# One weight sum of the gate-and-up product taken from two transfers: a plain load and an accumulating load

## The chip, the cores and the metric

The kernel runs on one core of one Trainium2 chip, as one program. The metric is the device time of that program in microseconds (us), measured on the chip. The profile used below is one separately profiled execution; times in it count from the start of its span. Its names for the engines are PE (TensorE, the matmul engine), DVE (VectorE), ACT (ScalarE), POOL (GpSimd) and SP (SyncE, which in this kernel issues the transfers between DRAM and on-chip memory).

## The reference

One layer of a hybrid encoder over 512 tokens of width 2048. The first part (two mixers behind one input projection, an output projection) is not touched by the change. The second part is a SwiGLU feed-forward network with 5632 hidden columns:

```python
h = rms_norm(x, norm2_g[layer]) * (1.0 + sc2) + sh2
gate, up = jnp.split(h @ w_ffn_in[layer], 2, axis=-1)
x = x + g2 * ((jax.nn.silu(gate) * up) @ w_ffn_out[layer])
```

All values are float32. `w_ffn_in` is 2048 by 11264: 5632 gate columns and 5632 up columns.

## The kernel before

Every matmul operand is split into a high part, which the matmul takes exactly, and a low part, the remainder (`S.copy` makes the high part on ScalarE, `V.tensor_sub` the low part on VectorE); a product is three matmuls per 128 rows of the contraction: high by high, high by low, low by high.

The first feed-forward product works on tiles f = 0 to 43 of 128 gate columns and the 128 up columns that belong to them. Tiles 0 and 1 are made in the plain way. Tiles 2 to 43 (lines 1004 to 1036) use a seven-product scheme of the Strassen-Winograd kind: the weights of a tile are four blocks of 1024 rows by 128 columns, A11 and A12 (gate, lower and upper half of the 2048 rows) and A21 and A22 (up, the same halves). On chip each is a tile of 128 partitions by 1024 values, 512 KB. Four sums of them are needed: S1 = A21 + A22, then A11 - A21 (kept in A21's place), S1 - A11 (kept in A11's place), and A12 minus that (in A12's place). The matching sums of the activations are made once, ahead of the loop (opA to opD in the profile).

The seven products of a tile run on TensorE in a fixed order, 24 matmuls of 128 by 256 each. In the profile they are told by their weights: ff_1 (A11 as loaded), ff_2 (A12 as loaded), ff_6 (S1 - A11), ff_7 (A11 - A21), ff_5 (S1), ff_4 (A22), ff_3 (the fourth sum). Each needs its weights split by `operand` (lines 880 to 886: ScalarE's cast at L884 makes ff_6h, VectorE's subtraction at L885 makes ff_6l). High and low parts have three buffers each, so a cast waits until the product three before it has been multiplied. Results are combined on VectorE (L1029, L1031, L1032, L990) and stored to DRAM by `keep` (L994, `actd`) for the second feed-forward product (`fo` in the profile).

Loads are issued by SP, in one queue and in order; `load_block` (L888 to 891) is the load of one block. A11 and A12 come from a pool of four buffers ("raw"), shared with the modulation weights (`ada`, L176) that are reduced on VectorE beside the first 16 or so tiles. A21, A22 and S1 come from a pool of five buffers ("raw2"). A transfer into a buffer waits on SP until the buffer's last user is done, and whatever stands behind it in SP's queue waits too.

The order on each engine is not the order of the code: a list scheduler of the framework places the instructions by priority and its own estimates of when operands are there, and gives out the buffers. The high-priority block moves splits and sums 300 steps ahead. The order that results is fixed in the program: an engine whose next instruction waits lets nothing pass.

Of the kernel before, what the change touches and what calls it, by code (L numbers as in the profile page):

```python
# [15 lines left out]
ALU = mybir.AluOpType  # L16
# [3 lines left out]
KT = 16  # L20
# [5 lines left out]
HALF = 8  # L26
# [102 lines left out]
def trunk(ctx, tc, a):  # L129
    nc = tc.nc  # L130
    V, S, G = nc.vector, nc.scalar, nc.gpsimd
# [11 lines left out]
    def acc(name):  # L143
        return psum.tile([P, T], F32, tag="acc", name=name)

    def att(name):
        return psum.tile([P, T], F32, tag="att", name=name, bufs=2)
# [732 lines left out]
    def operand(raw, name):  # L880
        hi = wp.tile([P, HALF, P], F32R, tag="hi", name=name + "h")
        lo = wp.tile([P, HALF, P], F32R, tag="lo", name=name + "l")
        with tc.high_priority(offset=AHEAD):
            S.copy(hi, raw)  # L884
            V.tensor_sub(lo, raw, hi.bitcast(F32))  # L885
        return hi, lo

    def load_block(pool, tag, bufs, f, g, kh):  # L888
        r = pool.tile([P, HALF, P], F32, tag=tag, name=f"ff{f}_{g}{kh}", bufs=bufs)
        nc.sync.dma_start(r, a["w_fi"][f, g][:, kh * HALF:kh * HALF + HALF])  # L890
        return r

    def product(out, w, p, first=False):
        whi, wlo = w
        for j in range(HALF):
            PE.matmul(out, whi[:, j], H[p][:, j, 0], start=first and j == 0, stop=False, skip_group_check=True)
            PE.matmul(out, whi[:, j], H[p][:, j, 1], start=False, stop=False, skip_group_check=True)
            PE.matmul(out, wlo[:, j], H[p][:, j, 0], start=False, stop=j == HALF - 1, skip_group_check=True)
# [83 lines left out]
    def tap(src, name):  # L982
        t = tp.tile([P, HT], F32, tag="tap", name=name, bufs=4)
        S.copy(t, src)
        return t
# [3 lines left out]
    def keep(f, sg, up):  # L989
        V.tensor_mul(sg, sg, up)  # L990
        pair = tp.tile([P, 2, T], F32R, tag="pair", name=f"pair{f}")
        S.copy(pair[:, 0], sg)
        V.tensor_sub(pair[:, 1], sg, pair[:, 0].bitcast(F32))
        nc.sync.dma_start(actd[f], pair.bitcast(F32))  # L994
# [9 lines left out]
    for f in range(2, FM):  # L1004
        A11, A12 = (load_block(wp, "raw", 4, f, 0, kh) for kh in range(2))
        A21, A22 = (load_block(tp, "raw2", 5, f, 1, kh) for kh in range(2))
        S1 = tp.tile([P, HALF, P], F32, tag="raw2", name=f"ffS{f}", bufs=5)
        A, B, C = acc(f"ffA{f}")[:, 0:HT], acc(f"ffB{f}")[:, 0:HT], att(f"ffC{f}")[:, 0:HT]
        w1, w2 = operand(A11, f"ff{f}_1"), operand(A12, f"ff{f}_2")
        with tc.high_priority(offset=AHEAD):  # L1010
            V.tensor_add(S1, A21, A22)
            V.tensor_sub(A21, A11, A21)
            V.tensor_sub(A11, S1, A11)
            V.tensor_sub(A12, A12, A11)
        product(A, w1, 1, True)
        ta = tap(A, f"a{f}")
        product(B, w2, 2, True)
        product(A, operand(A11, f"ff{f}_6"), 6)
        tb = tap(A, f"b{f}")
        product(C, operand(A21, f"ff{f}_7"), 7, True)  # L1020
        t_c = tap(C, f"c{f}")
        product(A, operand(S1, f"ff{f}_5"), 5)
        tu = tap(A, f"u{f}")
        product(C, operand(A22, f"ff{f}_4"), 4)
        product(A, operand(A12, f"ff{f}_3"), 3)

        sg = tp.tile([P, T], F32, tag="sg", name=f"sg{f}")
        up = tp.tile([P, T], F32, tag="up", name=f"up{f}")
        V.tensor_add(sg[:, 0:HT], B, ta)  # L1029
        S.activation(sg[:, 0:HT], sg[:, 0:HT], AF.Silu)  # L1030
        V.tensor_add(up[:, HT:T], tu, t_c)  # L1031
        V.tensor_add(up[:, 0:HT], C, tb)  # L1032
        S.activation(sg[:, HT:T], A, AF.Silu)
        keep(f, sg, up)
        if rest:
            rest.pop(0)()
# [98 lines left out]
```

## Time and profile before

| what | value |
|---|---|
| time, median of 2 runs | 2404.47 us (2404.03 to 2404.9) |
| the profiled execution's own time | 2405.08 us |
| its span | 2403.3 us |
| TensorE busy | 2321.8 us, 97% of the span |
| VectorE busy | 1701.3 us, 71% |
| ScalarE busy | 1033.9 us, 43% |
| GpSimd busy | 82.6 us, 3% |
| transfers, mean over the span | 168 GB/s |

The loop of tiles 2 to 43 lies between about 1067 us and 1921 us of the span. Busy time is time in which an engine had an instruction running; matmuls overlap, so their busy time alone does not tell how fast they run. An entry such as `<-DMA ff<-in_w_fi` behind an idle time names what ended it. In the chain of waits, followed back from the last instruction, each piece of time is given to the engine that it was spent on. "us to landing" of a transfer is the median time from its issue to its arrival. In the lists of order further below, the bracket names the counters for which an instruction waits: DMAHW for transfers issued by SP, DMASW for those issued by GpSimd, the others for engines.

### The profile page before, as it was taken

To read this page: it belongs to the slowest core of one execution; us is meant where nothing else is said; L and a number is where in the kernel's file an instruction comes from. 1 tells how busy PE (TensorE), PEld (TensorE's weight loads), DVE (VectorE), ACT (ScalarE), POOL (GpSimd) and SP (SyncE) were. 2 spreads that over 40 slices of the span, in tenths; PEclk is the share of its full clock that TensorE was granted. 3 is DMA by queue.
4 is the path that set the end of the run, shared out by engine and by line. 5 is a ranking of instruction groups with operands and counts; after the bars stand their busy time and mean duration, and the time that the engine had idled before them with its cause. 6 is when DMAs were issued, how large, how long until landed. Compare 5 with 4: busy or idle time off the path is not lost.

```text
span 2403.3 us, 36514 instructions
## 1 busy us (share of the span) xinstructions
PE 2321.8 (97%) x14371; PEld 2106.9 (88%) x14371; DVE 1701.3 (71%) x2585; ACT 1033.9 (43%) x1833; POOL 82.6 (3%) x64
## 2 busy tenths in 40 slices
PE   7989898999999999989999999999999999999999
PEld 6778788978888778889999999999999988888887
DVE  8997888789888875598888877777777633333332
ACT  4343664466565522374444444444444421122221
POOL 2250000000000200000000000000000000000000
PEclk9999999999999999999999999999999999999999
DMA  8878546743332286535555533333333484363342
GB/s 316 278 248 262 191 156 224 238 165 115 106 106 97 79 266 219 188 121 178 185 184 185 182 135 131 129 130 130 131 132 132 170 327 155 101 198 95 106 127 88
DMA packets 122488, 403.10 MB, mean 168 GB/s; under 512 B 13614, under 2 KB 14284, under 8 KB 122188
## 3 DMA queue, kind: packets, MB, share of 16 engines
q1 hardware_dynamic: 122316, 400.77, 49.8%
q8 instruction: 112, 1.84, 0.3%
q14 instruction: 60, 0.49, 0.1%
HBM read 369.24 MB, written 31.47 MB: 167 GB/s over the span
## 4 chain that ended last, share of the span: by engine, by line
PE 75%; DVE 10%; DMA 9%; issue 3%; ACT 2%; POOL 0%; POOLq 0%; SPq 0%; ACTq 0%; DVEq 0%
PE ffA L92 20%; PE fo L92 20%; PE ffC L92 10%; PE wo L92 6%; PE ffB L92 5%; DMA ada<-in_w_ada 4%; PE hgg L92 3%; DVE ada L183 3%; PE hgf L92 3%; PE hgq L92 3%; PE ff L92 1%; DMA fix<-in_w_fix 1%; DVE I L413 1%; PE l L92 1%; PE hgo L92 1%
## 5 line engine op out<-in xcount | busy, mean ns | idle before, releaser
L183 DVE SCALAR_TENSOR_TENSOR ada<-ada,cond 128x1024 f32<-128x1024 f32 x192 | 260.5, 1366 | 94.9 <-DMA ada<-in_w_ada 94.6
L92 PE MATMUL fo<-act,wfo_0h 128*128 128x512 f32 x1024 | 315.4, 389 | 0.0
L92 PEld LDWEIGHTS fo<-act,wfo_0h 128*128 128x128 f32 x1024 | 192.2, 188 | 39.9
L92 PE MATMUL fo<-act,wfo_0l 128*128 128x512 f32 x512 | 199.2, 389 | 0.0
L204 DVE TENSOR_TENSOR wfo_8l<-wfo_8r,wfo_8h 128x512 fp32r<-128x512 f32 x48 | 33.2, 692 | 177.6 <-ACT wfo_8h L203 177.6
L1071 DVE SCALAR_TENSOR_TENSOR x<-fo,mod,x 128x512 f32<-128x512 f32 x64 | 48.1, 751 | 131.2 <-PE fo L92 127.2
L203 ACT CAST wfo_0h<-wfo_0r 128x1024 fp32r<-128x1024 f32 x64 | 67.7, 1058 | 164.9 <-PE fo L92 142.1
L92 PE MATMUL ffA<-opA,ff_1h 128*128 128x256 f32 x672 | 124.6, 286 | 6.1 <-DVE up L1001 6.1
L92 PE MATMUL ffA<-opB,ff_6h 128*128 128x256 f32 x672 | 124.0, 285 | 2.1 <-ACT ff_6h L884 2.1
L92 PE MATMUL ffC<-opB,ff_7h 128*128 128x256 f32 x672 | 123.1, 283 | 0.4 <-ACT ff_7h L884 0.4
L92 PE MATMUL ffB<-opA,ff_2h 128*128 128x256 f32 x672 | 122.8, 283 | 0.0
L92 PE MATMUL ffA<-opC,ff_5h 128*128 128x256 f32 x672 | 122.8, 283 | 0.0
L92 PE MATMUL ffC<-opC,ff_4h 128*128 128x256 f32 x672 | 122.8, 283 | 0.0
L92 PE MATMUL ffA<-opD,ff_3h 128*128 128x256 f32 x672 | 122.8, 283 | 0.0
L203 ACT CAST wfo_8h<-wfo_8r 128x512 fp32r<-128x512 f32 x48 | 30.0, 624 | 210.3 <-PE fo L92 210.3
L92 PE MATMUL fo<-act,wfo_8h 128*128 128x512 f32 x384 | 118.2, 389 | 0.0
L92 PEld LDWEIGHTS fo<-act,wfo_0l 128*128 128x128 f32 x512 | 96.1, 188 | 19.9
L92 PEld LDWEIGHTS ffA<-opA,ff_1h 128*128 128x128 f32 x672 | 106.4, 195 | 6.3 <-issue 6.3
L92 PEld LDWEIGHTS ffA<-opB,ff_6h 128*128 128x128 f32 x672 | 105.9, 194 | 2.3 <-ACT ff_6h L884 2.3
L92 PEld LDWEIGHTS ffC<-opB,ff_7h 128*128 128x128 f32 x672 | 104.9, 192 | 0.7 <-ACT ff_7h L884 0.7
L92 PEld LDWEIGHTS ffB<-opA,ff_2h 128*128 128x128 f32 x672 | 104.8, 192 | 0.0
L92 PEld LDWEIGHTS ffA<-opC,ff_5h 128*128 128x128 f32 x672 | 104.8, 192 | 0.0
(691 smaller groups left out, 6727.1 us busy)
## 6 DMA issues: line engine op xcount, KB each, us to landing
ada<-in_w_ada SPq DMA_DIRECT2D x192, 512.0 KB, 4.5
ff<-in_w_fi SPq DMA_DIRECT2D x168, 512.0 KB, 3.6
wfo_0r<-in_w_fo SPq DMA_DIRECT2D x64, 512.0 KB, 3.6
actd<-pair SPq DMA_DIRECT2D x44, 512.0 KB, 2.6
act<-actd SPq DMA_DIRECT2D x44, 512.0 KB, 6.2
fix<-in_w_fix SPq DMA_DIRECT2D x28, 512.0 KB, 4.9
wfo_8r<-in_w_fo SPq DMA_DIRECT2D x48, 256.0 KB, 2.7
wo_8r<-in_w_out SPq DMA_DIRECT2D x16, 512.0 KB, 4.4
```

The lines of the kernel that those rows point to most:

```text
L92: self.engine.matmul(out, lhsT, rhs, **kw)
L183: V.scalar_tensor_tensor(w, w, 1.0, row[:, sl], op0=ALU.mult, op1=ALU.mult, accum_out=col)
L203: S.copy(hi, r)
L204: V.tensor_sub(lo, r, hi.bitcast(F32))
L413: V.tensor_tensor_scan(Ig[:, ::-1], seg[:, base:base + width][:, ::-1], Lg[:, ::-1], 0.0, op0=ALU.mult, op1=ALU.add)
L1071: V.scalar_tensor_tensor(x2[m], out, mcol(G2, m), x2[m], op0=ALU.mult, op1=ALU.add)
```

## The change

S1 is no longer added on VectorE. SP loads the upper half A22 from DRAM into S1's buffer a second time, and GpSimd then issues a transfer of the lower half A21 from DRAM that is added to what stands in that buffer. A21 and A22 are still loaded as before, for ff_7 and ff_4.

```diff
         A11, A12 = (load_block(wp, "raw", 4, f, 0, kh) for kh in range(2))
         A21, A22 = (load_block(tp, "raw2", 5, f, 1, kh) for kh in range(2))
         S1 = tp.tile([P, HALF, P], F32, tag="raw2", name=f"ffS{f}", bufs=5)
+        nc.sync.dma_start(S1, a["w_fi"][f, 1][:, HALF:KT])
+        nc.gpsimd.dma_start(S1, a["w_fi"][f, 1][:, 0:HALF], accum_op=ALU.add)
         A, B, C = acc(f"ffA{f}")[:, 0:HT], acc(f"ffB{f}")[:, 0:HT], att(f"ffC{f}")[:, 0:HT]
         w1, w2 = operand(A11, f"ff{f}_1"), operand(A12, f"ff{f}_2")
         with tc.high_priority(offset=AHEAD):
-            V.tensor_add(S1, A21, A22)
             V.tensor_sub(A21, A11, A21)
             V.tensor_sub(A11, S1, A11)
             V.tensor_sub(A12, A12, A11)
```

Lines behind the new ones move by one: the sum S1 - A11 is L1013 before and L1014 after, A11 - A21 is L1012 before and L1013 after.

The lists below are for VectorE and SP at one place well inside the loop, where no `ada` loads are left. Names: ff_00, ff_01, ff_10, ff_11 are A11, A12, A21, A22; ffS is S1; the number behind a name belongs to its tile f.

SP before, from one tile's first block to the next but one:

```order
L890 DMA ff_00_17489<-in_w_fi 128x1024 [waits DMAHW7_49,DVE_49]
L890 DMA ff_10_17493<-in_w_fi 128x1024 [waits DMAHW1_49,DVE_49]
L890 DMA ff_11_17495<-in_w_fi 128x1024 [waits DMAHW2_49,DVE_49]
L890 DMA ff_01_17491<-in_w_fi 128x1024 [waits DMAHW3_49,DVE_49]
L890 DMA ff_00_17721<-in_w_fi 128x1024 [waits DMAHW4_49,DVE_49]
L994 DMA actd_9457<-pair_17253 128x1024 [waits DMAHW5_49,DVE_49]
L890 DMA ff_10_17725<-in_w_fi 128x1024 [waits DMAHW6_49,DVE_49]
L890 DMA ff_11_17727<-in_w_fi 128x1024 [waits DMAHW7_49,DVE_49]
```

SP now, the same place:

```order
L890 DMA ff_10_17527<-in_w_fi 128x1024 [waits DMAHW3_49,DMASW0_49,DVE_49]
L890 DMA ff_11_17529<-in_w_fi 128x1024 [waits DMAHW4_49,DVE_49]
L890 DMA ff_01_17525<-in_w_fi 128x1024 [waits DMAHW5_49,DVE_49]
L890 DMA ff_00_17756<-in_w_fi 128x1024 [waits DMAHW6_49,DVE_49]
L1008 DMA ffS_17531<-in_w_fi 128x1024 [waits DMAHW7_49,DVE_49]
L994 DMA actd_9457<-pair_17286 128x1024 [waits DMAHW0_49,DVE_49]
L890 DMA ff_10_17760<-in_w_fi 128x1024 [waits DMAHW1_49,DMASW1_49,DVE_49]
L890 DMA ff_11_17762<-in_w_fi 128x1024 [waits DMAHW2_49,DVE_49]
```

The load of S1 has come in ahead of the store `actd`, and it waits for VectorE: its buffer is the one that A21 of the tile before held. The load of A21 (ff_10) now also waits for a GpSimd transfer, since its buffer held an S1. GpSimd's queue holds nothing in the loop but the accumulating transfers, each waiting for its own tile's S1 load and for the buffer.

VectorE before, from one tile's ff_7l to ff_2l of the next:

```order
L885 TENSOR_TENSOR ff_7l<-ff_10_17261,ff_7h 128x1024 [waits PE_49,Activation_49]
L993 TENSOR_TENSOR pair_17253<-sg_17245,pair_17253 128x512 [waits DMAHW3_49,Activation_49]
L1011 TENSOR_TENSOR ffS_17497<-ff_10_17493,ff_11_17495 128x1024 [waits DMAHW2_49,DMAHW1_49,DVE_49]
L1029 TENSOR_TENSOR sg_17477<-ffB_17267,a_17305 128x256 [waits PE_49,Activation_49]
L885 TENSOR_TENSOR ff_5l<-ffS_17265,ff_5h 128x1024 [waits Activation_49]
L1012 TENSOR_TENSOR ff_10_17493<-ff_00_17489,ff_10_17493 128x1024 [waits DMAHW7_49,DVE_49]
L885 TENSOR_TENSOR ff_4l<-ff_11_17263,ff_4h 128x1024 [waits PE_49,Activation_49]
L885 TENSOR_TENSOR ff_3l<-ff_01_17259,ff_3h 128x1024 [waits PE_49,Activation_49]
L885 TENSOR_TENSOR ff_1l<-ff_00_17489,ff_1h 128x1024 [waits PE_49,Activation_49]
L1031 TENSOR_TENSOR up_17478<-u_17419,c_17389 128x256 [waits Activation_49]
L1013 TENSOR_TENSOR ff_00_17489<-ffS_17497,ff_00_17489 128x1024 [waits DVE_49]
L1032 TENSOR_TENSOR up_17478<-ffC_17268,b_17359 128x256 [waits PE_49]
```

VectorE now, the same stretch without its first two rows, up to ff_2l:

```order
L1030 TENSOR_TENSOR sg_17511<-ffB_17302,a_17339 128x256 [waits PE_49,Activation_49]
L885 TENSOR_TENSOR ff_5l<-ffS_17298,ff_5h 128x1024 [waits Activation_49]
L885 TENSOR_TENSOR ff_4l<-ff_11_17296,ff_4h 128x1024 [waits DMAHW6_49,PE_49,Activation_49]
L1013 TENSOR_TENSOR ff_10_17760<-ff_00_17756,ff_10_17760 128x1024 [waits DMAHW6_49,DMAHW1_49,DVE_49]
L885 TENSOR_TENSOR ff_3l<-ff_01_17292,ff_3h 128x1024 [waits PE_49,Activation_49]
L885 TENSOR_TENSOR ff_1l<-ff_00_17523,ff_1h 128x1024 [waits PE_49,Activation_49]
L1032 TENSOR_TENSOR up_17512<-u_17453,c_17423 128x256 [waits Activation_49]
L1014 TENSOR_TENSOR ff_00_17523<-ffS_17531,ff_00_17523 128x1024 [waits DMASW2_49,DVE_49]
L1033 TENSOR_TENSOR up_17512<-ffC_17303,b_17393 128x256 [waits PE_49]
L885 TENSOR_TENSOR ff_2l<-ff_01_17525,ff_2h 128x1024 [waits DMAHW5_49,Activation_49]
```

The addition is gone. S1 - A11 keeps its place behind ff_1l and ahead of ff_2l and now waits for the accumulating transfer of the same tile. A11 - A21 has moved: it stands between ff_4l and ff_3l, and it is that of the tile after the next (17756, while ff_4l and ff_3l are of 17290), so it waits for the load ff_10_17760 of the list of SP. So it stands in 25 tiles; beside the `ada` loads it stands behind ff_1l. The order on TensorE is unchanged, and that on ScalarE but for one instruction.

## The prediction

> **What bounds the kernel now.** I read the busy times first, then the chain of waits for the whole span, then the busy times stretch by stretch. The page, the first line of its part 1 and the first of its part 4:
>
> ```profile
> PE 2321.8 (97%) x14371; PEld 2106.9 (88%) x14371; DVE 1701.3 (71%) x2585; ACT 1033.9 (43%) x1833; POOL 82.6 (3%) x64
> PE 75%; DVE 10%; DMA 9%; issue 3%; ACT 2%; POOL 0%; POOLq 0%; SPq 0%; ACTq 0%; DVEq 0%
> ```
>
> Two stretches of the loop (columns: stretch, its length, then busy time and instructions of PE, PEld, DVE, ACT, POOL, then granted clock, share of the DMA engines, GB/s), and at the end the stretch in which `fo` starts, the busiest for transfers:
>
> ```profile
> 1140.00:1400.00 260.00, 260.00 (x2169) 260.00 (x2168) 224.55 (x268) 124.64 (x180) 0.00 (x0) 1.00 0.53 180
> 1400.00:1900.00 500.00, 500.00 (x4169) 500.00 (x4168) 377.53 (x397) 239.29 (x348) 0.00 (x0) 1.00 0.38 130
> 1920.00:1960.00 40.00, 40.00 (x181) 33.24 (x180) 15.36 (x18) 9.33 (x10) 0.00 (x0) 1.00 0.98 374
> ```
>
> TensorE is busy in all 260 of 260 and 500 of 500 us, at full clock. VectorE is at 86% in the first stretch (with `ada`) and 76% in the second, GpSimd at nothing, the DMA engines at half and less. That TensorE is not only busy but paced by its own work is told by the chain of one tile (start, length, piece):
>
> ```profile
> 1701.87 2.88 PE ffB L92 x24
> 1704.75 2.88 PE ffA L92 x24
> 1707.63 2.88 PE ffC L92 x24
> 1710.51 2.88 PE ffA L92 x24
> 1713.39 2.88 PE ffC L92 x24
> 1716.27 5.76 PE ffA L92 x48
> 1722.03 2.88 PE ffB L92 x24
> ```
>
> Seven products of 2.88 us are 20.16 us, and 1722.03 - 1701.87 is 20.16: no gap is left. Taking work off VectorE can shorten nothing here. What is left are the waits at the start of the loop (TensorE's first matmul of three products, with the idle time before it and what ended it):
>
> ```profile
> 1067.29 0.76 PE L92 MATMUL ffA<-opA,ff_1h 128*128 128x256 f32 x2 [6.08 <-DVE up L1001]
> 1077.18 0.50 PE L92 MATMUL ffA<-opB,ff_6h 128*128 128x256 f32 x2 [2.06 <-ACT ff_6h L884]
> 1078.12 0.66 PE L92 MATMUL ffC<-opB,ff_7h 128*128 128x256 f32 x2 [0.45 <-ACT ff_7h L884]
> ```
>
> Their sum, 8.6 us or 0.36% of the time, is all that this stage can give.
>
> **What is removed.** 42 additions of S1, a row of the tile ffS (min/median/max in ns):
>
> ```profile
> L1011 DVE TENSOR_TENSOR ffS<-ff,ff x42: 1216/1217/1224, 1071.3 to 1886.1; 128x1024 f32<-128x1024 f32 x42
> ```
>
> 42 x 1.22 = 51 us of VectorE's 1701.3. Worth 0 on the path, by the two stretches above; only the one at 1071.3 lies in the chain (below). The instruction that read A22 first on VectorE is gone too; ScalarE's cast of ff_4 now waits for that load itself, a tile later, at no cost.
>
> **What is added inside the loop.** Two transfers of 512 KB per tile, one behind the other, since the second adds to what the first wrote. VectorE and SP around one tile change (engine, line, operation; the number after the start is the length):
>
> ```profile
> 1702.92 1.23 DVE L885 TENSOR_TENSOR ff_7l<-ff,ff_7h 128x1024 fp32r<-128x1024 f32 x1 [1.06 <-ACT ff_7h L884]
> 1706.13 1.21 DVE L885 TENSOR_TENSOR ff_5l<-ffS,ff_5h 128x1024 fp32r<-128x1024 f32 x1
> 1708.63 1.23 DVE L885 TENSOR_TENSOR ff_4l<-ff,ff_4h 128x1024 fp32r<-128x1024 f32 x1
> 1711.56 1.23 DVE L885 TENSOR_TENSOR ff_3l<-ff,ff_3h 128x1024 fp32r<-128x1024 f32 x1 [1.71 <-ACT ff_3h L884]
> 1715.86 1.22 DVE L1013 TENSOR_TENSOR ff<-ffS,ff 128x1024 f32<-128x1024 f32 x1
> 1717.00 0.42 DVE L1032 TENSOR_TENSOR up<-ffC,b 128x256 f32<-128x256 f32 x1
> 1717.33 1.21 DVE L885 TENSOR_TENSOR ff_2l<-ff,ff_2h 128x1024 fp32r<-128x1024 f32 x1
> 1704.77 0.33 SPq L994 DMA_DIRECT2D actd<-pair  x1
> 1707.38 0.33 SPq L890 DMA_DIRECT2D ff<-in_w_fi  x1
> ```
>
> Landing times of 512 KB, the first two from 1700 to 1742 us, the third from the whole page, where many loads run at once:
>
> ```profile
> ff<-in_w_fi SPq DMA_DIRECT2D x9, 512.0 KB, 3.5
> actd<-pair SPq DMA_DIRECT2D x2, 512.0 KB, 2.6
> act<-actd SPq DMA_DIRECT2D x44, 512.0 KB, 6.2
> ```
>
> *When S1's load can start.* Its buffer was A21 of the tile before, last read by ff_7l, which ends at 1702.92 + 1.23 = 1704.15. SP issues it then, ahead of `actd` (1704.77), which does not become later than its own pair makes it. A load takes 3.5 us, with 0.3 for the store beside it: in at 1708.0.
>
> *The accumulating transfer, L2.* No row shows one; GpSimd issues none before. From below it costs a store's 2.6 us. From above, reading and writing both at the pace of the crowded loads, 2 x 6.2 = 12.4 us. I take 7.0, two loads of 3.5 in series, since it moves every byte in, adds it, and has idle DMA engines more often than crowded ones: S1 is complete at 1715.0.
>
> The Trainium skill, "DMA: Bandwidth & Descriptors", section "Anatomy of one DMA — SWDGE (gpsimd) path", gives about 2.0 us and 436 GB/s for a transfer issued by GpSimd, which for 512 KB would be an estimate of 3.2 us, and S1 complete at 1711.2; no run here shows it, and the fit is for plain loads. [...]
>
> *When it is needed.* S1 - A11 stands today at 1715.86, so 0.9 us is left before anything moves at all. Behind it in VectorE's queue stand upC (0.33 to the next start) and ff_2l; TensorE takes up ff_2 at 1722.03. Latest start of S1 - A11: 1722.03 - 1.14 - 0.33 - 1.21 = 1719.35. So L2 may be 1719.35 - 1708.0 = 11.3 us. Below that the cost is 0; above, each tile becomes longer by the excess, since the next load of S1 starts from the ff_7l that was delayed: 41 us per us.
>
> *What else is queued.* In 25 tiles A11 - A21 now stands ahead of ff_3l and waits for the A21 load issued at 1707.38: in at 1710.9, the subtraction (1.14 to the next start) done at 1712.0, ff_3l 0.5 us later than today's 1711.56. TensorE takes up ff_3 at 1716.27; the load may take 1716.27 - 1.23 - 1.14 - 1707.38 = 6.5 us. Its bounds are 3.5 and, beside the accumulating transfer, 6.2. Cost 0, with little room. In the tiles with `ada` it stands behind ff_1l, where its load has long landed.
>
> *Traffic.* A tile adds 2 x 0.524 MB in 20.16 us, 52 GB/s, or 78 if the accumulating transfer counts twice: 180 becomes 232 to 258, 130 becomes 182 to 208, under the 374 that the engines moved at 0.98. SP's issue time (0.33 us each) is 2% of a tile.
>
> **What is added at the start of the loop.** There the sum lies on the path (chain, start and length):
>
> ```profile
> 1061.31 4.37 DVE opC L857 x13
> 1066.13 5.12 DMA ff<-in_w_fi
> 1071.35 1.22 DVE ffS L1011
> 1073.17 1.14 DVE ff L1012
> 1074.91 1.13 DVE ff L1013
> 1077.51 0.57 DVE ff_6l L885
> ```
>
> A21 and A22 land at 1071.25, since their buffers come free at 1061.31 + 4.37 = 1065.7. S1's load is third in that queue; 512 KB at 374 GB/s are 1.4 us more, so 1072.7 to 1073. With L2 = 7.0 S1 is in at 1080, S1 - A11 done at 1081.1 instead of 1076.05: **+5 us** for ff_6 on TensorE. With L2 from 2.6 to 12.4 it is 0.7 to 10.5. GpSimd's first transfer waits for that load alone by then, its earlier work being long over.
>
> **Sum.** 2405.08 (the profiled execution, its span of 2403.3 and 1.8 around it) - 0 + 0 + 5 = 2410.1; the median of the timed runs lies 0.6 lower, so 2409.5 for a median: I say 2409, +0.2%.
>
> **The rivals.** (1) *The accumulating transfer is too slow and VectorE's wait on it becomes the pace.* For: it stands in front of ff_2l in a queue in order, and the bound of 12.4 exceeds the 11.3 allowed. Against: DMA engines are idle half the loop. At 12.4: 41 x 1.1 = 45 us, and 10 at the start, 2460; from L2 = 12.2 the change costs over 2%. 15 us would give 2404.5 + 152 + 13 = 2570. Chance 0.15. (2) *Loads get in each other's way in part of the tiles*, mostly A21's load ahead of ff_3l, when it takes 7.5 instead of 3.5 to 6.2 us: 25 x 1.0 = 25 us, with the start 2435 (2415 to 2450). For: from 1704 to 1710 four transfers overlap where two did. Chance 0.18. (3) *It comes out level or a little faster:* L2 of 3 us or less, and VectorE, rid of the first addition, is early at the start. At best the 2.5 us at ff_6 and ff_7 go: 2402 to 2405. Chance 0.06. The change doing nothing is no rival, since the additions are gone from VectorE's order.
>
> **How the numbers follow.** My forecast, no stall but the start, 2405 to 2415, has 0.61. Time 2409. The range from 2403 to 2455 takes in the forecast, rival 2 and the near end of rival 1, and leaves out most of rival 1 and a little of rival 3. A measurement of this kernel tells about 2% from no change, 48 us: faster by that is out of reach (8.6 us at most), 0.01; slower is rival 1 and a small part of rival 2, 0.17; within is the rest, 0.82.
>
> **What would show it.** GpSimd's transfers in the list of DMA issues, at 512 KB and about 7 us to landing. In the stretches 1140 to 1400 and 1400 to 1900 TensorE still busy throughout, VectorE lower by 1.22 x 260 / 20.16 = 16 and 30 us. At the start, TensorE's wait for ff_6 grown from 2.06 to about 7 us. I am wrong if VectorE's line 1014 shows idle time ended by a GpSimd transfer in most tiles and TensorE waits for ff_2 (rival 1), or if line 1013 waits for a load and TensorE for ff_3 (rival 2).

## The result, and the profile after

The changed kernel takes 2485.85 us (median of 2 runs, 2482.29 to 2489.41) against 2404.47 us: a ratio of 1.0339, with a 95% interval from 1.0312 to 1.0365. It is 3.4% slower; 2409 was predicted, with a range that ended at 2455. The profiled execution took 2489.41 us, with a span of 2487.6 us, 84.3 us more than before.

The page of the changed kernel: busy times, the chain of waits, and transfers (KB each, median us to landing):

```profile
PE 2351.6 (95%) x14371; PEld 2127.4 (86%) x14371; DVE 1651.1 (66%) x2543; ACT 1030.7 (41%) x1833; POOL 119.1 (5%) x106
...
PE 59%; DMA 18%; DVE 15%; issue 5%; ACT 2%; POOL 0%; SPq 0%; DVEq 0%; ACTq 0%; POOLq 0%
...
ff<-in_w_fi SPq DMA_DIRECT2D x168, 512.0 KB, 5.7
...
actd<-pair SPq DMA_DIRECT2D x44, 512.0 KB, 6.0
...
ffS<-in_w_fi SPq DMA_DIRECT2D x42, 512.0 KB, 5.3
ffS<-in_w_fi POOLq DMA_DIRECT2D x42, 512.0 KB, 7.7
```

VectorE is rid of its 50 us of additions, and TensorE's share of the chain falls from 75% to 59%: transfers and VectorE now hold a third of the path. The accumulating transfer lands after 7.7 us, close to the 7.0 that was assumed. But the weight loads, at 3.6 us before, take 5.7, and the store `actd`, at 2.6, takes 6.0 (medians over the whole program).

The same stretches of the changed kernel as before (stretch, length, busy time of PE, PEld, DVE, ACT, POOL, granted clock, DMA share, GB/s):

```profile
1140.00:1400.00 260.00, 230.77 (x1823) 226.92 (x1822) 176.36 (x215) 101.72 (x151) 9.46 (x11) 0.97 0.65 201
1400.00:1900.00 500.00, 489.36 (x4010) 485.30 (x4010) 340.02 (x371) 231.44 (x336) 20.71 (x24) 0.99 0.62 181
```

TensorE was busy 260 of 260 us; now it is 230.77, with a sixth fewer matmuls in the same time (1823 for 2169). The loss is above all in the tiles with `ada`.

A finer account follows from the starts of ff_2 on TensorE, tile by tile. Before, the first interval between two starts is 24.83 us and each of the other 40 is 20.16. In the changed kernel the last ff_2 starts 83.9 us later than before, nearly the whole 84.3, and the parts are:

| part of the program | what the changed kernel takes longer |
|---|---|
| up to the first ff_2 | 4.0 us |
| first interval | 7.0 us |
| the next 15, with `ada` loads | 62.5 us, 4.2 each (22.0 to 27.5 us instead of 20.16) |
| the last 25 | 10.5 us, 0.42 each |

The cause of the first row stays open: in the profiles below it scatters from -3.6 to +5.8 us. The other three are the subject of the runs.

TensorE's waits and those of VectorE's two sums in the changed kernel, in the loop (us in all, how often, the longest):

```profile
DVE ff L1013 <- DMA ff<-in_w_fi: 119.6, 38, 5.0
DVE ff L1014 <- DMA ffS<-in_w_fi: 60.0, 28, 6.8
PE ffA L92 <- ACT a L984: 28.4, 22, 2.0
PE ffB L92 <- DVE ff_2l L885: 20.7, 13, 5.6
PE ffA L92 <- ACT ff_6h L884: 9.4, 1, 9.4
```

Line 1013 is A11 - A21, line 1014 is S1 - A11. The prediction named line 1014's wait on the accumulating transfer as the danger; line 1013's wait for a plain load is twice as long. Line 1014's wait came in 28 of the 42 tiles and TensorE's wait for ff_2l in 13, so the sign of rival 1 showed in part.

One tile with `ada` shows what that does. TensorE in the changed kernel, where ff_2 of one tile starts, its two waits, and the next ff_2:

```profile
1206.58 0.40 PE L92 MATMUL ffB<-opA,ff_2h 128*128 128x256 f32 x2
...
1208.93 0.39 PE L92 MATMUL ffB<-opA,ff_2l 128*128 128x256 f32 x1 [1.95 <-DVE ff_2l L885]
...
1213.59 0.50 PE L92 MATMUL ffA<-opB,ff_6h 128*128 128x256 f32 x2 [1.77 <-ACT a L984]
...
1230.96 0.40 PE L92 MATMUL ffB<-opA,ff_2h 128*128 128x256 f32 x2
```

VectorE, SP and GpSimd in the same tile, in order of time (start, length, engine, line, operation, and the idle time before it):

```profile
1218.75 0.86 POOL L1009 DMA_DIRECT2D ffS<-in_w_fi  x1 [23.09 <-DMA ffS<-in_w_fi]
...
1220.83 1.23 DVE L183 SCALAR_TENSOR_TENSOR ada<-ada,cond 128x1024 f32<-128x1024 f32 x1 [0.75 <-DMA ada<-in_w_ada]
...
1222.09 0.33 SPq L890 DMA_DIRECT2D ff<-in_w_fi  x1
...
1223.53 1.23 DVE L885 TENSOR_TENSOR ff_1l<-ff,ff_1h 128x1024 fp32r<-128x1024 f32 x1 [0.20 <-ACT ff_1h L884]
1229.50 1.23 DVE L1013 TENSOR_TENSOR ff<-ff,ff 128x1024 f32<-128x1024 f32 x1 [4.75 <-DMA ff<-in_w_fi]
1230.65 1.22 DVE L1014 TENSOR_TENSOR ff<-ffS,ff 128x1024 f32<-128x1024 f32 x1
1231.78 1.22 DVE L885 TENSOR_TENSOR ff_2l<-ff,ff_2h 128x1024 fp32r<-128x1024 f32 x1
```

1230.96 - 1206.58 is 24.38 us, 4.22 over the old pace, and the two waits are 1.95 + 1.77 = 3.72 of it. The load issued at 1222.09 is the block A11 of the tile after the next. Its buffer belongs to the pool shared with `ada`, and comes free when line 183 has read the `ada` block, at 1220.83 + 1.23 = 1222.06. It lands 7.4 us later, and that is when A11 - A21 of that far tile starts, 1229.50. This subtraction has stood first in VectorE's queue since ff_1l ended at 1224.76, with nothing that anyone needs soon; behind it stand S1 - A11 and ff_2l, which TensorE needs now. S1 itself was there: 1218.75 + 8.3 (the landing time of that transfer) is 1227.0.

The load of A11 is issued within 0.05 us of the end of a read of `ada` in 14 tiles in a row, from 1125 to 1440 us. No run gives A11 a buffer of its own, so the part of the shared buffer is read from the trace and not tested.

In the late tiles the sums stand differently. SP, GpSimd and VectorE of the changed kernel from 1700 to 1716 us:

```profile
1700.25 0.33 SPq L1008 DMA_DIRECT2D ffS<-in_w_fi  x1
...
1706.27 0.86 POOL L1009 DMA_DIRECT2D ffS<-in_w_fi  x1 [19.95 <-DMA ffS<-in_w_fi]
...
1708.35 1.23 DVE L1013 TENSOR_TENSOR ff<-ff,ff 128x1024 f32<-128x1024 f32 x1 [2.91 <-DMA ff<-in_w_fi]
...
1713.56 1.23 DVE L1014 TENSOR_TENSOR ff<-ffS,ff 128x1024 f32<-128x1024 f32 x1 [1.38 <-DMA ffS<-in_w_fi]
```

Here S1 - A11 waits for the accumulating transfer itself, which GpSimd issues 6.0 us after SP issued the load, and which is in 7.3 us later. This one is just in time for the products behind it. The longest such wait of the late tiles is not (chain of waits of the changed kernel: start, length, piece):

```profile
1781.84 5.51 DMA ffS<-in_w_fi
...
1787.90 9.25 DMA ffS<-in_w_fi
...
1797.24 0.10 DVE ff L1014
...
1798.39 0.42 DVE up L1033
...
1802.33 0.61 DVE sg L990
...
1803.49 0.37 ACT a L984
...
1803.91 2.17 PE ffA L92 x16
```

The late S1 reaches TensorE by a path that the prediction did not price: upC (line 1033) behind S1 - A11, the product of line 990, ScalarE's cast of the pair, and behind that in ScalarE's queue the copy of `a` that frees the accumulator ffA for ff_6. ff_2 started at 1799.06 in that tile, so ff_6 was due at 1801.94; it starts at 1803.91, and the tile takes 22.22 us.

This chain closes on itself, into a cycle with one turn a tile. The buffer for the next S1 comes free when VectorE has made ff_7l, which stands behind S1 - A11 in its queue: here it ends at 1804.07, 6.83 us after S1 - A11 started, and the next load of S1 is issued at 1804.09, 22.25 us behind the one of 1781.84. From that load's issue to the landing of the sum it is 15.31 us, to the start of S1 - A11 0.09, to the end of ff_7l 6.83, to the next issue 0.02: together this turn is as long as the tile.

### The profile page after: what moved, and what is told of

Same layout as the page of the kernel before. It is cut to its first block, busy times and chain, and to the rows that moved or that the text cites. A ratio compares the mean times of both kernels' runs of the same rounds, so it can differ in the third digit from the quotient of the medians.

```text
span 2487.6 us, 36702 instructions
## 1 busy us (share of the span) xinstructions
PE 2351.6 (95%) x14371; PEld 2127.4 (86%) x14371; DVE 1651.1 (66%) x2543; ACT 1030.7 (41%) x1833; POOL 119.1 (5%) x106
## 4 chain that ended last, share of the span: by engine, by line
PE 59%; DMA 18%; DVE 15%; issue 5%; ACT 2%; POOL 0%; SPq 0%; DVEq 0%; ACTq 0%; POOLq 0%
PE fo L92 19%; PE ffA L92 13%; DMA ada<-in_w_ada 8%; PE ffC L92 6%; PE wo L92 4%; DVE ada L183 4%; PE hgg L92 3%; PE hgf L92 3%; DMA ffS<-in_w_fi 3%; PE hgq L92 3%; DMA ff<-in_w_fi 3%; PE ffB L92 2%; PE ff L92 1%; DMA fix<-in_w_fix 1%; DVE ff_6l L885 1%
## 5 line engine op out<-in xcount | busy, mean ns | idle before, releaser
L92 PE MATMUL ffA<-opB,ff_6h 128*128 128x256 f32 x672 | 135.5, 302 | 37.9 <-ACT a L984 28.4
L92 PEld LDWEIGHTS ffA<-opB,ff_6h 128*128 128x128 f32 x672 | 112.3, 206 | 44.2 <-ACT a L984 34.3
L1013 DVE TENSOR_TENSOR ff<-ff,ff 128x1024 f32<-128x1024 f32 x42 | 51.4, 1225 | 119.6 <-DMA ff<-in_w_fi 119.6
L92 PE MATMUL ffB<-opA,ff_2l 128*128 128x256 f32 x336 | 97.7, 291 | 20.7 <-DVE ff_2l L885 20.7
```

Of the source, the lines that this page charges most:

```text
L92: self.engine.matmul(out, lhsT, rhs, **kw)
```

## The experiments

Two explanations stood at the outset. **The order:** with the addition gone from VectorE, the framework's scheduler put A11 - A21 a tile further ahead, where it waits for loads in front of urgent work. **The traffic:** 52 GB/s more, part of it written by a GpSimd transfer, slows the loads. After the first four runs a third one joined them, **the late sum:** two transfers in series are too long from the moment when S1's buffer comes free. The expectations stand as they were written at the time; theory A in them is the order. The kernel before, timed on the same chip, took 2404.63 us beside runs 1 to 4, 2407.57 beside 5, 6, 8 and 9, and 2404.61 beside run 7. The ratios are against these. What start (the first interval), tiles with `ada` and late tiles take longer is counted as in the table above, from one profile of each kernel.

**1. The order put back.** A11 - A21 is made to be issued behind the previous tile's ff_5l, about where it stood before. This moves lines down, by 3 from A11 - A21 on (S1 - A11 is line 1017). The first line of the cut stands in `operand`, which now keeps the low-part subtractions by name in `lows`.

```diff
-            V.tensor_sub(lo, raw, hi.bitcast(F32))
+            lows[name] = V.tensor_sub(lo, raw, hi.bitcast(F32))
...
-            V.tensor_sub(A21, A11, A21)
+            with tc.issue_after(lows[f"ff{f - 1}_5"].ins) if f > 2 else nullcontext():
+                V.tensor_sub(A21, A11, A21)
```

> The changed kernel with one instruction held back on VectorE: A11 - A21 of a tile may not be issued before the ff_5l of the tile before, which puts it back to one tile ahead, as in the kernel before. Both transfers for S1 stay. Theory A (the moved subtraction: in the tiles with ada it stands ahead of S1 - A11 and ff_2l and waits for A11's load of the tile after the next, issued only after ff_3l because its buffer was ada's): tiles with ada go back from 24.3 us to 20.2 to 20.8, late tiles stay at about 20.6 because S1 itself still lands 13 us after its load is issued; 2415 to 2430 us. Theory B (the added traffic and the slow accumulating transfer hold up everything): tiles with ada stay near 24 us, 2465 us or more.

Measured: 2447.43 us, ratio 1.0182 (1.0156 to 1.0208). Start 8.7 us, tiles with `ada` 20.4, late tiles 11.5. VectorE in the loop of this kernel:

```profile
DVE ff L1017 <- DMA ffS<-in_w_fi: 107.2, 42, 7.4
```

Putting the order back takes away two thirds of the loss beside `ada`, 42 of 62.5 us, and nothing of the late tiles. What remains is the late sum: now line 1017 waits for it in each of the 42 tiles. The time was above what the order alone allows, and I had to add the third explanation.

The remaining loss is the cycle described above. One turn of it in this kernel:

```profile
1202.01 0.33 SPq L1010 DMA_DIRECT2D ffS<-in_w_fi  x1
...
1215.90 1.23 DVE L1017 TENSOR_TENSOR ff<-ffS,ff 128x1024 f32<-128x1024 f32 x1 [2.51 <-DMA ffS<-in_w_fi]
...
1221.51 1.22 DVE L887 TENSOR_TENSOR ff_7l<-ff,ff_7h 128x1024 fp32r<-128x1024 f32 x1
...
1222.76 0.33 SPq L1010 DMA_DIRECT2D ffS<-in_w_fi  x1
```

S1 - A11 starts when S1 is in, ff_7l ends 6.83 us later at 1222.73, and the next load of S1 goes out at 1222.76. From the issue of S1's load to the landing of its sum it is 14.45 us in the median beside `ada` and 13.67 in the late tiles; with 6.94 for the rest of the cycle (0.09, 6.82 and 0.03) that is 21.4 and 20.6 us, and the tiles take 21.5 and 20.6 in the mean.

Edit 1 puts back more than A11 - A21. Beside `ada` the changed order also has the two sums `up` behind ff_2l and behind ff_6l, where the kernel before and this one have them ahead of S1 - A11 and of ff_2l. From S1 - A11 to the end of ff_7l the changed kernel takes 7.22 us there and this one 6.82, so they are worth about 0.4 us a tile, an estimate, or 6 of the 42 us. The order below means all three moves; no run parts them.

**2. The order kept, no accumulating transfer.** S1 then holds A22 alone.

```diff
         nc.sync.dma_start(S1, a["w_fi"][f, 1][:, HALF:KT])
-        nc.gpsimd.dma_start(S1, a["w_fi"][f, 1][:, 0:HALF], accum_op=ALU.add)
```

> The changed kernel without its accumulating transfer: S1 is only the plain load of A22, so the lower-half summand of S1 is left out of the result. The order on VectorE stays that of the changed kernel in all but the first tiles. Theory A: VectorE still waits for A11's load ahead of S1 - A11; with one transfer less per tile that load is faster (about 5 us instead of 7), tiles with ada 21.5 to 23 us, 2430 to 2455 us in all. Theory B: S1 is there 8 us earlier and half of the added traffic is gone: tiles 20.2 to 20.5 us, 2405 to 2415 us.

Measured: 2422.62 us, ratio 1.008 (1.0064 to 1.0097). Tiles with `ada` 20.6 us longer, late tiles 0.0, start 3.2 shorter. VectorE in this kernel (lines lie one higher, so line 1012 is A11 - A21 and line 1013 is S1 - A11), over the loop:

```profile
DVE ff L1012 <- DMA ff<-in_w_fi: 80.7, 40, 3.3
PE ffA L92 <- ACT a L984: 15.1, 14, 1.8
...
DVE ff L1013 <- DMA ffS<-in_w_fi: 0.2, 1, 0.2
```

The moved subtraction costs 20.6 us without any transfer of GpSimd, and without a wait for S1: it is a cause by itself, of the size that the late sum has beside `ada`. In the late tiles it waits too and costs nothing. The time is below what theory A gave, which had put the whole loss on the order, and above theory B's.

**3. The traffic alone, a first form.** The kernel before, untouched, with the same two transfers into a buffer that nobody reads.

```diff
+        J1 = tp.tile([P, HALF, P], F32, tag="junk", name=f"ffJ{f}", bufs=1)
+        nc.sync.dma_start(J1, a["w_fi"][f, 1][:, HALF:KT])
+        nc.gpsimd.dma_start(J1, a["w_fi"][f, 1][:, 0:HALF], accum_op=ALU.add)
```

> The kernel before, S1 added on VectorE, with the same two transfers per tile (plain load and accumulating transfer) into a buffer that nobody reads. Traffic without the new waits and with A11 - A21 one tile ahead. Theory A: tiles stay at 20.16 to 20.4 us, 2405 to 2418 us. Theory B: loads of 512 KB lengthen as in the changed kernel and tiles with ada go to 22 us and more, 2440 us or more.

Measured: 2556.4 us, ratio 1.0627 (1.0609 to 1.0644), far off every expectation and slower than the change itself. Start -0.5 us, tiles with `ada` 141.3, late 11.8. SP's queue in this kernel, from 1100 to 1450 us, where line 1009 is the unused load, and VectorE in the whole loop:

```profile
SPq L1009 <- DMA ffJ<-in_w_fi: 234.8, 29, 11.4
```

```profile
DVE ada L183 <- DMA ada<-in_w_ada: 161.1, 21, 11.1
```

The unused load waits on SP for the accumulating transfer of the tile before, and the `ada` and weight loads queue behind it. So this form put a new wait into SP's queue, and it says nothing on traffic alone.

**4. The GpSimd transfer made plain.** Order and transfers as in the change, but the second transfer overwrites instead of adding (S1 holds A21 alone).

```diff
-        nc.gpsimd.dma_start(S1, a["w_fi"][f, 1][:, 0:HALF], accum_op=ALU.add)
+        nc.gpsimd.dma_start(S1, a["w_fi"][f, 1][:, 0:HALF])
```

> The changed kernel with the second transfer into S1, from GpSimd, made a plain one (it overwrites instead of adding, so S1 is A21 alone; the upper-half summand is left out). Same order, same waits, same number of transfers. It measures what adding costs inside a transfer. If the add needs a second read of every byte, the landing falls from 7.7 us to 4 to 5 us and late tiles go to 20.16 to 20.3 us; if the time lies in GpSimd's issue and the queueing, it stays at 7 us or more. Theory A: tiles with ada stay above 22 us either way, 2450 to 2485 us. Theory B: 2405 to 2430 us if the landing falls.

Measured: 2442.57 us, ratio 1.0162 (1.0147 to 1.0178). Start 4.6 us, tiles with `ada` 35.4, late 0.0. The transfers of this kernel:

```profile
ffS<-in_w_fi SPq DMA_DIRECT2D x42, 512.0 KB, 4.4
ffS<-in_w_fi POOLq DMA_DIRECT2D x42, 512.0 KB, 6.8
```

With adding the transfer takes 7.7 - 6.8 = 0.9 us more in the median (8.2 against 6.0 beside `ada`, 7.6 against 7.0 in the late tiles), and the load before it 0.9 us more as well. These 1.8 us make 27 us of the tiles with `ada` and all of the late ones: S1 stands at the edge, where single microseconds decide. In the late tiles of this kernel the sum lands 12.1 us after the load's issue, which fits into the 20.16 - 6.94 = 13.2 that the cycle leaves. The landing stayed near 7 us, the expectation's second case, but the late tiles went to 20.16 us, which was tied to the first. The time is below the range of theory A, which left the accumulation no part in it, and above theory B's.

**5. Order put back and no accumulating transfer** (edits 1 and 2 together).

> The changed kernel with A11 - A21 held back to one tile ahead and without the accumulating transfer (S1 is the plain load of A22 alone, the lower-half summand is left out). With the earlier runs it fills a square: order moved or put back, accumulating transfer there or not. Theory A+B (either the moved subtraction costs, or the late S1, and with both away nothing is left): tiles with ada 20.16 to 20.3 us, late tiles 20.16, 2400 to 2408 us. Theory C (the extra load of S1 as traffic costs by itself beside the ada loads): tiles with ada stay at 21.3 us as without the accumulating transfer alone, about 2420 us.

Measured: 2405.31 us, ratio 0.9983 (0.9967 to 0.9999). Start 3.1 us shorter, tiles with `ada` 0.0, late 0.0. So the additional load on SP, half the added traffic, costs nothing, and edit 1 removes the whole price of the order.

**6. Order put back and a sixth buffer** for A21, A22 and S1, so that S1's load need not wait for the previous tile's ff_7l. The whole sum is made, with both transfers.

```diff
-        A21, A22 = (load_block(tp, "raw2", 5, f, 1, kh) for kh in range(2))
-        S1 = tp.tile([P, HALF, P], F32, tag="raw2", name=f"ffS{f}", bufs=5)
+        A21, A22 = (load_block(tp, "raw2", 6, f, 1, kh) for kh in range(2))
+        S1 = tp.tile([P, HALF, P], F32, tag="raw2", name=f"ffS{f}", bufs=6)
```

> The changed kernel with A11 - A21 held back to one tile ahead and six buffers instead of five for A21, A22 and S1, so that S1's load need not wait for the ff_7l of the tile before. Theory B (with the order put back, what is left of the loss, 20 us in the tiles with ada and 11 in the late ones, is S1 landing later than its turn): late tiles 20.16 us, tiles with ada 20.16 to 20.5, only the start of the loop (+7 to +9 us) stays; 2408 to 2418 us. Theory C (traffic): tiles with ada stay at 21.4 us; 2425 to 2435 us.

Measured: 2413.56 us, ratio 1.0027 (1.0011 to 1.0043). Start 7.2 us, tiles with `ada` 0.0, late 0.0. Two stretches of this kernel:

```profile
1140.00:1400.00 260.00, 260.00 (x2169) 260.00 (x2168) 211.48 (x256) 124.48 (x182) 11.19 (x13) 1.00 0.77 234
1400.00:1900.00 500.00, 500.00 (x4169) 500.00 (x4169) 355.00 (x374) 236.26 (x348) 21.57 (x25) 1.00 0.63 182
```

TensorE is busy throughout again, with all the added traffic in place, 234 GB/s instead of 180. VectorE is lower by 13 and 23 us, where 16 and 30 were predicted. What the predicted profile should have shown is here, and nearly the predicted cost: 6.0 us over the kernel before beside it, where 5 were predicted. With the cycle opened by one buffer, the late sum costs nothing.

**7. The sixth buffer alone**, the moved order kept (in the late tiles A11 - A21 stands in front of ff_4l here).

> The changed kernel with six buffers instead of five for A21, A22 and S1 and nothing else: S1 can be loaded early, but A11 - A21 still stands two tiles ahead, in front of S1 - A11 in the tiles with ada (in the late tiles it stands ahead of ff_4l here). Theory A+B as two separate waits: the late tiles go to 20.16 us as with the order put back; the tiles with ada keep the cost of the moved subtraction alone, about 20 us in all as without the accumulating transfer, so 2425 to 2440 us with the start. If six buffers take the cost of the moved subtraction away too, 2408 to 2418 us, then the late S1 was the only cause; if the tiles with ada stay at 24 us, 2470 us or more, S1's lateness had no part in them.

Measured: 2436.86 us, ratio 1.0122 (1.0094 to 1.0151). Start 8.8 us, tiles with `ada` 21.4, late 0.0. This kernel's waits in the loop:

```profile
DVE ff L1013 <- DMA ff<-in_w_fi: 65.6, 38, 2.6
...
PE ffA L92 <- ACT a L984: 15.4, 13, 1.8
...
DVE ff L1014 <- DMA ffS<-in_w_fi: 7.7, 1, 7.7
```

S1 is late once, at the start. The late sum is cured, and the order's 21 us stay, as without the accumulating transfer (20.6). With runs 1, 2 and 6 the four corners are complete, in the tiles with `ada`:

| | S1 late | S1 early or not accumulated |
|---|---|---|
| A11 - A21 moved ahead | 62.5 (the change) | 20.6 and 21.4 |
| A11 - A21 put back | 20.4 | 0.0 and 0.0 |

Together they cost 21 us more than their sum. The cycle shows why. In the changed kernel S1 - A11 stands behind A11 - A21, so that the wait for A11 becomes a part of the cycle: in the tile shown above S1 is in at 1227.0, and S1 - A11 starts only at 1230.65. Over the tiles with `ada`, the medians are 13.7 us from the issue of S1's load to the landing of the sum, 2.9 from there to S1 - A11, and 7.2 to the end of ff_7l, 23.8 in all; the tiles take 24.3 in the mean. Where the cycle has room or is open (runs 2 and 7) the same order costs a third of that.

The wait for A11 is also longer in the changed kernel: over the fifteen intervals with `ada` line 1013 waits 48.0 us, against 24.0 in run 7 and 21.7 for the same subtraction in run 2. The load takes 6.5 us there in the median, 4.5 in run 7 and 4.1 in run 2, and the accumulating transfer runs beside it for 4.5, 1.8 and 0 us. In the tile above the load of A11 is issued 3.3 us behind the accumulating transfer; in run 7 it goes first, at 1204.54, with the transfer at 1206.87, and takes 4.8 us. That the one slows the other agrees in all three kernels, but no run tests it by itself.

**8. The traffic alone, paced.** As run 3, but the unused load is issued behind the same tile's load of A11 and so does not go ahead of the tiles' own (`load_block` keeps each load in `issued`).

```diff
+        J1 = tp.tile([P, HALF, P], F32, tag="junk", name=f"ffJ{f}", bufs=1)
+        with tc.issue_after(issued[f, 0, 0].ins):
+            nc.sync.dma_start(J1, a["w_fi"][f, 1][:, HALF:KT])
+        nc.gpsimd.dma_start(J1, a["w_fi"][f, 1][:, 0:HALF], accum_op=ALU.add)
```

> The kernel before with the same two transfers per tile (plain load, then accumulating transfer) into a buffer that nobody reads, now issued at the pace of the tiles: the plain load is queued behind that tile's load of A11. Theory A+B: nobody waits for them, tiles 20.16 to 20.4 us, 2404 to 2412 us. Theory C (traffic): the loads get slower and the tiles with ada longer by about 1.3 us each, 2420 to 2435 us.

Measured: 2414.48 us, ratio 1.0031 (1.0014 to 1.0049). Start -0.3 us, tiles with `ada` 3.5, late 0.0. Of this kernel a stretch, and the transfers:

```profile
1140.00:1400.00 260.00, 259.11 (x2152) 258.29 (x2152) 222.35 (x266) 124.33 (x179) 11.19 (x13) 1.00 0.78 235
```

```profile
ff<-in_w_fi SPq DMA_DIRECT2D x168, 512.0 KB, 5.4
...
ffJ<-in_w_fi POOLq DMA_DIRECT2D x42, 512.0 KB, 6.5
```

The weight loads slow from 3.6 to 5.4 us, nearly as much as in the change (5.7), and the old order bears it at 3.5 us in this profile. The profiled execution is the fastest of the ten; the median is 6.9 us above the kernel before and lies between the two ranges. So the traffic by itself costs from 3 to 12 us, by the interval, of the change's 81, and is not the main cause; it lengthens the loads for which the new order waits.

**9. The best of it.** Run 6, and the first tile's S1 added on VectorE as before. The cut is against run 6:

```diff
-        nc.sync.dma_start(S1, a["w_fi"][f, 1][:, HALF:KT])
-        nc.gpsimd.dma_start(S1, a["w_fi"][f, 1][:, 0:HALF], accum_op=ALU.add)
+        if f > 2:
+            nc.sync.dma_start(S1, a["w_fi"][f, 1][:, HALF:KT])
+        if f > 2:
+            nc.gpsimd.dma_start(S1, a["w_fi"][f, 1][:, 0:HALF], accum_op=ALU.add)
...
+            if f == 2:
+                V.tensor_add(S1, A21, A22)
```

> The changed kernel with A11 - A21 held back, six buffers, and the sum of the first tile (f = 2) made by VectorE as before, so that the start of the loop has no second transfer behind the first. Theory B: nothing is left of the loss, 2402 to 2410 us, and no gain over the kernel before since TensorE sets the pace. Theory C: 2418 us or more.

Measured: 2410.55 us, ratio 1.0008 (0.9989 to 1.0026). The first interval is back at 0.0, the next one 3.5 us longer, the rest 0.0; the cause of the 3.5 was not followed. The time is 0.55 us above theory B's range. So the start's price came from the two transfers of the first S1; with the first of them alone (runs 2 and 5) the start is 3 us shorter than before. These 3 us are about all that the addition was worth. No version that makes the whole sum beats the kernel before: TensorE paces it.

## Why the prediction was wrong

**What bounds the kernel, and what the removal is worth: right.** VectorE was relieved of 1701.3 - 1651.1 = 50 us, predicted 51, and no stretch became shorter. Runs 5 and 6, with the additions gone and the waits cured, are at the old pace of 20.16 us to the hundredth.

**The step that failed: "In the tiles with `ada` it stands behind ff_1l, where its load has long landed."** I looked at the load of A21, which is issued first, and not at the other operand, A11. In these tiles A11's load is issued when an `ada` block has been read from the shared buffer, in the tile shown 5.0 us behind A21's (1217.12 and 1222.09), and it lands 4.75 us after VectorE came to it. The list of order showed the instruction two tiles ahead, and its operands' loads could have been followed on SP. The step was worth 0 in the sum; it costs 20.6 us by itself (run 2), and 42 us on top of the late S1 (62.5 less the 20.4 of run 1), both with the two sums `up` that moved along.

**S1's chain inside the loop: terms near, limit wrong.** This step, "So L2 may be 1719.35 - 1708.0 = 11.3 us. Below that the cost is 0", failed as well. The accumulating transfer, 7.0 assumed, took 7.7 in the median, between the bounds of 2.6 and 12.4 and under the limit of 11.3. S1's load, 3.8 assumed, took 5.3, and from its landing to GpSimd's issue there is about half a microsecond more (0.55 in the chain shown), which the sum did not have. Together that is 13.5 instead of 10.8, in a limit of 3.8 + 11.3 = 15.1, and it still cost 20.4 + 11.5 us beyond the start (run 1).

The limit was too wide because it was counted to TensorE's use of ff_2 in one tile. I did say that the next load of S1 starts from a delayed ff_7l, but not that this ff_7l stands only 6.8 us behind S1 - A11 on VectorE. Round the cycle, 20.16 - 6.94 leaves 13.2 us from the issue of S1's load to the landing of the sum, or 9.4 for the accumulating transfer behind a load of 3.8. Run 1 has 13.67 in the late tiles and 14.45 beside `ada`, and pays about the excess in the mean; run 4 has 12.1 in the late tiles and pays nothing there; run 6 opens the cycle and pays nothing in either.

By the fit of the Trainium skill, "DMA: Bandwidth & Descriptors", section "Anatomy of one DMA — SWDGE (gpsimd) path", about 2.0 us and the bytes at 436 GB/s, 512 KB from GpSimd would take an estimate of 3.2 us. Run 4, where GpSimd's transfer is plain, has 6.8 in the median, beside the other loads of the loop; no run here has such a transfer by itself.

**A11 - A21 in the late tiles: right, with less room than thought.** It waits there 2.9 us in the tile shown, in front of ff_3l, and TensorE does not wait for ff_3. Run 2 has this order in all late tiles at 0.0.

**Traffic: the rates right, the landing times not.** 234 and 182 GB/s at full pace (run 6) are the lower ends of 232 to 258 and 182 to 208. But the loads went from 3.6 to 5.4 us with the traffic alone (run 8) and to 5.7 in the change, where the sum had 0.3 for the store.

**The start: mechanism right, 7 us for 5.** TensorE's wait for ff_6 grew from 2.06 to 9.40 us, predicted about 7. The chain of the changed kernel there:

```profile
1077.17 8.91 DMA ffS<-in_w_fi
```

The accumulating transfer took 8.91 us for 7.0.

**The rivals.** None is what happened. Rival 1 is the late sum, and its place (line 1014, in front of ff_2l) was right, but it gave a cost only from an accumulating transfer of more than 11.3 us; at 7.7 it would have been nothing. Rival 2, loads in each other's way in part of the tiles, is nearest in kind. It put the price on ff_3l in the 25 late tiles, where the cost is 0, and its top of 2450 lies 36 us below the result. That the two would meet in the same tiles and cost more than their sum was in no case.

## What to carry to other kernels

When a change takes an instruction off an engine that was not the bound, look at what the scheduler puts into the hole: for each instruction that moved ahead, follow all its operands to the loads that bring them and to the buffers that these wait for, since in a queue in order a far-sighted instruction stalls urgent ones. When an operand comes in two transfers in series, follow its buffer all the way round, from the moment when it comes free to the moment when the work behind the sum frees it again; this cycle has to fit into one tile, whatever a single consumer allows. A buffer more, and one instruction held in place, left 6 of the changed kernel's 81 us here, and showed that there had been next to nothing to win.

## What the hardware showed

GpSimd's 512 KB took 6.5 to 8.0 us in the medians of the runs with the tiles' other loads beside them (5.6 in run 7), and adding instead of overwriting went with 0.9 us of that (run 4 against the change; 0.6 in the late tiles, 2.2 beside `ada`). A load on SP that waits for a GpSimd transfer stops every load behind it: 234.8 us of such waiting in run 3, and a kernel 6% slower from two transfers that nobody reads.

The granted clock, the share of TensorE's full clock that it was allowed, fell in stretches with waits: 0.97 in the changed kernel from 1140 to 1400 us, where TensorE is busy 89%, against 1.00 in run 6 (busy throughout) and in the kernel before. The fifteen intervals with `ada` of the changed kernel:

```profile
1107.88:1472.81 364.93, 321.24 (x2523) 315.63 (x2522) 250.61 (x303) 142.60 (x212) 12.91 (x15) 0.96 0.63 194
```

TensorE waits 43.7 us there and is busy 18.8 us longer than the 302.4 of fifteen tiles before, which makes up the 62.5. In run 1 the same intervals have a granted clock of 1.00, with single waits of at most 1.1 us instead of 5.6, and TensorE is busy 5.3 us longer. So most of the longer busy time goes with the lower clock. Whether that lengthened the tiles or only filled time in which TensorE would have waited is not shown; the cycle of S1 comes within half a microsecond of their length.
